# A two-layer diffusion trunk on one core: modulation weights in a ring of their own, and no pass called for at a feed-forward's turn

## The chip, the cores and the metric

One Trainium2 chip, and one core of it. The metric is the device time of one execution in microseconds, median over the runs. The engines go by the profile's names: PE is TensorE's matmuls and PEld its weight loads, DVE is VectorE, ACT ScalarE, POOL GpSimd, SP SyncE, whose queue issues the DMAs of the weights.

## What is computed

A latent stream of 256 tokens and a context of 256 tokens, 1024 channels each, go through two layers. A layer is a half-step feed-forward, four token mixers that are merged by gates, and another half-step feed-forward. Cut to what matters here:

```python
mod_x = (silu(c) @ w_ada[l] + b_ada[l]).reshape(c.shape[0], 1, 3, 3, D_MODEL)
mod_c = (silu(c_ctx) @ w_ada[l] + b_ada[l]).reshape(3, 3, D_MODEL)

def swiglu_ffn(h, w_in, w_out):
    a = h @ w_in
    return (silu(a[..., :D_FF]) * a[..., D_FF:]) @ w_out

def gated_merge(branches, pg, w_branch, w_out):
    ys = stack(branches, axis=2)
    proj = einsum('bnim,imd->bnid', ys, w_branch)
    gate = sigmoid(pg.reshape(B, N, N_BRANCH, D_MODEL))
    return sum(gate * proj, axis=2) @ w_out

x = residual(x, swiglu_ffn(modulate(x, mod_x, 0), ffn_w_in[l, 0], ffn_w_out[l, 0]), mod_x, 0, ...)
```

The modulation (`mod_x`, `mod_c`) is a product of two vectors with a matrix of 1024 x 9216 for each layer: shift, scale and gate of the three sub-layers. The sub-layers are called (l, s) below, with s = 0 for the first feed-forward, 1 for the mixers, 2 for the second feed-forward; feed-forwards are called (l, w).

## The kernel before

**Layout.** Channels lie on the partitions: eight tiles of 128 channels with 512 columns, 256 of the context and 256 of the latent stream. In layer 1 the second feed-forward and most of the mixers work on the latent columns alone.

**Matrix products in three terms.** Every operand is split into a high and a low part, and `mm3` (L149 and on) issues three matmuls: high times high, high times the low part of the activations, low part of the weights times high. `wload` loads a weight block of 128 x 1024 (`raw`), ACT makes `hi` from it (`split`, L125) and DVE makes `lo` (L113). Rings: four buffers for `raw`, six each for `hi` and `lo`. Products go into five banks of PSUM (`mm`) and three more (`ax`).

**Feed-forward** (`ffn`, from L524). The 22 blocks of the hidden layer are worked in three parts, `PARTS = ((0, 6), (6, 14), (14, 22))`. In each part the input tiles come first: two weight blocks per tile, 48 matmuls; then ACT makes silu (`sg`), DVE multiplies it by the other half (the product, `sg<-sg,mm`), ACT makes the high part (`gh<-sg`) and DVE the low part (`gh<-sg,gh`). This is called a gate below. Then come the eight output tiles over all gates of the part (`out_tiles`), each added to the residual stream by DVE (`ah<-mm,gate,ah`). The step from the last gate of a part to its first output tile is called a turn: turn 1 to 3. Output tile 0 needs the last gate last: PE works through the older gates of the part first.

**Mixer** (`mixer`, ends at L1165). In its last phase `merge` makes eight gated products for each of the four branches; for each of these 32, called a merge below, DVE multiplies (`th<-th,mm`) and adds (`mg<-mg,th`). Then the eight sums are split (`mh`, high part on ACT, low part on DVE), and the output projection (`o2`) follows.

**Modulation passes.** The modulation isn't done on PE but on DVE, beside the rest. `mods(l, s)` (from L206) is a generator: for each 128 rows of the modulation matrix it loads a block of 128 x 1024 (`ada`, L214) and makes two passes over it, one for each vector (`junk<-ada,cbc`, L216), a product with a running sum:

```python
w = wp.tile([128, D], F32, tag="raw", name=nm("ada"), bufs=4)
nc.sync.dma_start(w, I["wada"][l, s * 24 + t])
for v in range(2):
    V.tensor_tensor_reduce(out=cur["junk"], in0=w, in1=cur["c"][:, v], ...)
    yield
```

`pump(n)` takes n passes from the generators that are queued. `ffn` calls `pump(np_)` after each gate (L551) and `pump(nm_)` after each output tile (L561), with `PUMPS = ((3, 3), (3, 0), (3, 1))` for the feed-forwards (0,0), (0,1) and (1,0). Layer 0 has 112 passes, which go with feed-forward (0,0); layer 1 has 144, queued ahead of feed-forward (0,1); (1,1) has none. `ada` blocks share the ring of four with all weight blocks.

**What sets the order.** The code issues instructions in program order, but a scheduler of the framework then orders each engine's rows anew: a row may move ahead of others where nothing that it needs holds it (its buffer, its data). The queue of SP issues DMAs in its order, and a DMA waits there for its buffer to be free.

Of the kernel before, what the change touches and what calls it, by code (L numbers as in the profile page):

```python
# [10 lines left out]
F32 = mybir.dt.float32  # L11
# [5 lines left out]
D = 1024  # L17
# [43 lines left out]
def trunk_kernel(ctx: ExitStack, tc: tile.TileContext, I: dict, out: bass.AP):  # L61
# [71 lines left out]
            stt(out=lo, in0=src, scalar=scale, in1=hi.bitcast(F32), op0=ALU.mult, op1=ALU.subtract)  # L133

    def wload(ap, n=1024):
        raw = wp.tile([128, 1024], F32, tag="raw", name=nm("raw"), bufs=4)
        nc.sync.dma_start(raw[:, :n], ap)
        hi = wp.tile([128, 1024], F32R, tag="hi", name=nm("hi"), bufs=6)
        lo = wp.tile([128, 1024], F32R, tag="lo", name=nm("lo"), bufs=6)
        split(hi[:, :n], lo[:, :n], raw[:, :n])  # L140
        return hi, lo
# [65 lines left out]
    def mods(l, s):  # L207
        m = const.tile([128, 2, 24], F32, name=f"mod{l}{s}")
        mod[l, s] = m
        first = (l, s) == (0, 0)  # L210
        order = ([] if first else [c * 8 + k for k in range(8) for c in (1, 0)]) + [16 + k for k in range(8)]
        for n, t in enumerate(order):
            w = wp.tile([128, D], F32, tag="raw", name=nm("ada"), bufs=4)
            nc.sync.dma_start(w, I["wada"][l, s * 24 + t])  # L214
            for v in range(2):
                V.tensor_tensor_reduce(out=cur["junk"], in0=w, in1=cur["c"][:, v], scale=1.0, scalar=0.0,  # L216
                                       op0=ALU.mult, op1=ALU.add, accum_out=m[:, v, t:t + 1])
                yield
            if n == 15 and not first:
                g = const.tile([128, 2, 8], F32, name=f"gp{l}{s}")  # L220
                b = const.tile([128, 2, 8], F32, name=f"bp{l}{s}")
                pl, pk = (l, s - 1) if s else (l - 1, 2)
                for v in range(2):
                    sc, sh = m[:, v, 8:16], m[:, v, 0:8]
                    tt(out=sh, in0=sh, in1=col(l, "b_ada", s * 24, 8), op=ALU.add)
                    tt(out=sc, in0=sc, in1=col(l, "b_ada", s * 24 + 8, 8), op=ALU.add)
                    stt(out=g[:, v], in0=sc, scalar=1.0, in1=col(pl, "ln_g", pk * 8, 8), op0=ALU.add, op1=ALU.mult)
                    stt(out=b[:, v], in0=sc, scalar=1.0, in1=col(pl, "ln_b", pk * 8, 8), op0=ALU.add, op1=ALU.mult)
                    tt(out=b[:, v], in0=b[:, v], in1=sh, op=ALU.add)
                gp[l, s], bpc[l, s] = g, b  # L230
        gt = const.tile([128, 2, 8], F32, name=f"gate{l}{s}")
        for v in range(2):
            tt(out=gt[:, v], in0=m[:, v, 16:24], in1=col(l, "b_ada", s * 24 + 16, 8), op=ALU.add)
        if s != 1:
            ts(out=gt, in0=gt, scalar1=0.5, scalar2=None, op0=ALU.mult)
        gate[l, s] = gt
# [91 lines left out]
    def start(mid):  # L328


        xh, xl = xtiles()
        g = const.tile([128, 2, 8], F32, name="gp00")
        b = const.tile([128, 8, 2], F32, name="bp00")
        m = const.tile([128, 2, 8], F32, name="sc00")
        p = aux("shift")
        tiles, rows = [], None
        ws = {}

        def load(u):
            ws[u] = [blk("shw") for _ in range(4)]  # L340
            for i in range(4):
                nc.sync.dma_start(ws[u][i], I["wshift"][u, i])

        load(0)
        nc.sync.dma_start(cols[0], I["cols"][0])
        nc.sync.dma_start(pos, I["pos"])
        for u in range(4):
            wa = []
            for k in (2 * u, 2 * u + 1):
                wa.append(wp.tile([128, D], F32, tag="raw", name=nm("ada"), bufs=4))  # L350
                nc.sync.dma_start(wa[-1], I["wada"][0, 8 + k])
            for k in (2 * u, 2 * u + 1):
                nc.sync.dma_start(ah[k], I["xc"][k])
            if u < 3:
                load(u + 1)
            if u % 2 == 0:
                rows = aux("row")
            r = rows[0:2, (u % 2) * 256:(u % 2) * 256 + 256]
            for i in range(8):
                mm(r, ccol[:, i], ws[u][i // 2][:, (i % 2) * 256:(i % 2) * 256 + 256], start=i == 0, stop=i == 7)  # L360
            rs = blk("row")[0:2, 0:256]
            act(rs, r, AF.Copy)
            for k in (2 * u, 2 * u + 1):
                w = wa[k % 2]
                for v in range(2):
                    V.tensor_tensor_reduce(out=cur["junk"], in0=w, in1=cur["c"][:, v], scale=1.0, scalar=0.0,  # L366
                                           op0=ALU.mult, op1=ALU.add, accum_out=m[:, v, k:k + 1])
                ts(out=g[:, :, k], in0=m[:, :, k], scalar1=col(0, "b_ada", 8 + k), scalar2=1.0, op0=ALU.add, op1=ALU.add)
                mm(p[:, 2 * k:2 * k + 2], rs[:, (k % 2) * 128:(k % 2) * 128 + 128], ident[0:2, 0:2],
                                 start=True, stop=True)  # L370
                act(b[:, k], p[:, 2 * k:2 * k + 2], AF.Identity, bias=col(0, "b_ada", k))
                x3 = ah[k][:, T:].rearrange("p (r c) -> p r c", c=64)
                pk = (pos[:, 4 * k:4 * k + 4].rearrange("p (r c) -> p r c", c=1) if k < 4 else
                      pos[:, 16 + (k - 4) * 64:80 + (k - 4) * 64].rearrange("p (r c) -> p r c", r=1))
                G_.tensor_tensor(out=x3, in0=x3, in1=pk.to_broadcast([128, 4, 64]), op=ALU.add)
                xf = blk("xf")
                for v in range(2):
                    act(xf[:, vcols(v)], ah[k][:, vcols(v)], AF.Identity, scale=g[:, v, k:k + 1], bias=b[:, k, v:v + 1])
                split(xh[k], xl[k], xf)
            if u in MID:  # L380
                tiles += mid(MID.index(u))
        nc.sync.dma_start(masks, I["masks"].rearrange("d p t -> p d t"))
        nc.sync.dma_start(cols[1], I["cols"][1])
        for k in range(8):
            act(ah[k], ah[k], AF.Copy, scale=ALPHA)
        for l in range(DEPTH):
            for s in range(3):
                a = const.tile([128, 2, 8], F32, name=f"alg{l}{s}")
                ts(out=a[:, 0], in0=col(l, "ln_g", s * 8, 8), scalar1=ALPHA, scalar2=None, op0=ALU.mult)
                ts(out=a[:, 1], in0=col(l, "ln_b", s * 8, 8), scalar1=ALPHA, scalar2=None, op0=ALU.mult)  # L390
                alg[l, s] = a
        return xh, xl, tiles
# [118 lines left out]
    def first_tiles(n):  # L511
        if n < 2:
            return ffn_tiles(0, 0, (n,))
        tiles = []
        for h in range(2):
            raw = wp.tile([128, D], F32, tag="raw", name=nm("raw"), bufs=4)
            nc.sync.dma_start(raw, I["ffn_in"][0, 0, n, h])
            hi, lo = [blk("wh", F32R) for _ in range(2)], [blk("wl", F32R) for _ in range(2)]
            for i in range(2):
                split(hi[i], lo[i], raw[:, i * 512:i * 512 + 512])  # L520
            tiles.append((aux() if h else mmb(), hi, lo))
        return tiles

    def ffn(l, w, bd, first, cs, order, np_, nm_=1):  # L524
# [5 lines left out]
        for pi, (j0, j1) in enumerate(PARTS):  # L530
            gh, gl = [], []
            j = j0
            while j < j1:
# [9 lines left out]
                for i, jj in enumerate(js):  # L543
                    sg = blk("sg")
                    act(sg[:, cs], tiles[2 * i][0][:, cs], AF.Silu)
                    tt(out=sg[:, cs], in0=sg[:, cs], in1=tiles[2 * i + 1][0][:, cs], op=ALU.mult)
                    a, b = blk2("gh", cs, F32R)
                    split(a[:, cs], b[:, cs], sg[:, cs])
                    gh.append(a)
                    gl.append(b)  # L550
                    pump(np_)  # L551
                j += len(js)
            if pi == 0:
                finish_gate(l, s)
# [2 lines left out]
            def evac(m, p, c, vs):  # L557
                resid(m, p, l, s, vs)
                if fin:
                    nrm.arrive(m, c)  # L560
                pump(nm_)  # L561

            rest = out_tiles(lambda m: wload(I["ffn_out"][l, w, m, :, j0 * 128:j1 * 128], (j1 - j0) * 128),
                             gh, gl, cs, order, evac, LAG if fin and len(order) > 1 else 0)
# [9 lines left out]
    def mixer(l, bd, cs, sets, order):  # L574
# [44 lines left out]
        ready = {}  # L619

        def chunk(key):
            n = plan.index(key)
            for x in plan[n:n + 1 + AHEAD]:
                if x not in ready:
                    w = I["w_" + x[0]][l]
                    w = w[x[1] // 4, x[1] % 4] if x[0] == "br" else w[x[1]]
                    if plain(x):
                        ready[x] = wp.tile([128, 1024], F32, tag="raw", name=nm("raw"), bufs=4)
                        nc.sync.dma_start(ready[x], w)
                    else:  # L630
                        ready[x] = wload(w)
# [252 lines left out]

        def gates_v_in():

            raw = wp.tile([128, 1024], F32, tag="raw", name=nm("raw"), bufs=4)
            nc.sync.dma_start(raw[:, :128], I["w_gt"][l])
            hi = wp.tile([128, 1024], F32R, tag="hi", name=nm("hi"), bufs=6)
            lo = wp.tile([128, 1024], F32R, tag="lo", name=nm("lo"), bufs=6)  # L890
# [431 lines left out]
```

## Time and profile before

| | |
|---|---|
| runs, median (lowest to highest) | 2267.71 us (2266.44 to 2270.55) |
| profiled execution, its own time | 2267.27 us |
| its span | 2265.5 us |
| mean granted clock of TensorE | 0.991 |
| busy: PE, DVE, ACT | 98%, 72%, 42% of the span |
| DMA | 142 GB/s on the mean |

A busy time is the sum of an engine's instructions in a stretch. A wait stands at the instruction that waited, with the one that released it. The clock is the share of full speed that the chip granted to TensorE. One feed-forward with 512 columns takes some 370 us, and turn 2 of feed-forward (0,0) lies at 222 us in this execution.

### The profile page before, as it was taken

Reading aid. Unit: us, or ns where it says so; the run is one execution under the profiler, and the core shown is the slowest. Engines: PE = TensorE matmul, PEld = TensorE weight load, DVE = VectorE, ACT = ScalarE, POOL = GpSimd, SP = SyncE. Lnnn points to the kernel's source line nnn. Section 1 sums busy time; section 2 is a strip of 40 time slices with the busy share of each in tenths; the row PEclk is TensorE's granted clock in tenths of the full one; section 3 lists DMA queues with packets and bytes.
Section 4 is the critical chain, followed back from the end, with each engine's and each line's share of the span. In section 5 each row is a group of like instructions: output and inputs, shape, how many; then the busy total and the mean of one; then the engine's idle time right before and its main releaser. Section 6 shows DMA issues by size and latency. Waiting matters only on the chain.

```text
span 2265.5 us, 31565 instructions
## 1 busy us (share of the span) xinstructions
PE 2221.0 (98%) x12216; PEld 1908.4 (84%) x12216; DVE 1630.0 (72%) x2881; ACT 947.0 (42%) x1477; POOL 19.9 (1%) x82
## 2 busy tenths in 40 slices
PE   7999999999999999999999999999999999998997
PEld 4888788988888888898888888888889998998997
DVE  6998855768995754795746498766558988776656
ACT  5323123742345753362222254222226645755443
POOL 2000000000000000000000000000000000000000
PEclk9999999999999999999999999999999999999999
DMA  8676643223232132244545425554434543354652
GB/s 308 220 229 221 192 152 94 98 84 113 94 99 88 57 103 93 96 135 150 170 129 158 130 84 186 179 180 152 140 102 142 192 139 103 122 174 136 203 180 83
DMA packets 94454, 323.23 MB, mean 143 GB/s; under 512 B 10592, under 2 KB 12640, under 8 KB 94304
## 3 DMA queue, kind: packets, MB, share of 16 engines
q1 hardware_dynamic: 94304, 321.22, 43.9%
q8 instruction: 96, 1.57, 0.3%
q14 instruction: 54, 0.44, 0.1%
HBM read 320.12 MB, written 1.05 MB: 142 GB/s over the span
## 4 chain that ended last, share of the span: by engine, by line
PE 87%; DVE 7%; DMA 3%; issue 2%; ACT 2%; SPq 0%; DVEq 0%; ACTq 0%
PE mm L122 82%; DVE junk L216 2%; DMA ada<-in_wada 1%; DVE lo L113 1%; PE num L122 1%; DMA raw<-in_ffn_in 1%; DVE junk L366 1%; ACT hi L125 1%; DVE ah L113 0%; PE gt L122 0%; PE ax L122 0%; PE qk L122 0%; PE bcm L122 0%; PE bcr L122 0%; PE st L122 0%
## 5 line engine op out<-in xcount | busy, mean ns | idle before, releaser
L125 ACT ACTIVATE hi<-raw 128x1024 fp32r<-128x1024 f32 (+1 forms) x462 | 474.5, 1031 | 1040.0 <-PE mm L122 659.1
L122 PE MATMUL mm<-xh,hi 128*128 128x512 f32 (+1 forms) x2448 | 847.8, 349 | 5.0 <-ACT hi L125 3.0
L122 PE MATMUL mm<-xl,hi 128*128 128x512 f32 (+1 forms) x2448 | 850.0, 348 | 0.0
L122 PE MATMUL mm<-xh,lo 128*128 128x512 f32 (+1 forms) x2448 | 850.0, 348 | 0.0
L113 DVE TENSOR_TENSOR lo<-raw,hi 128x1024 fp32r<-128x1024 f32 (+1 forms) x462 | 546.2, 1185 | 264.6 <-ACT hi L125 262.4
L122 PEld LDWEIGHTS mm<-xh,hi 128*128 128x128 f32 x2448 | 462.4, 190 | 65.0 <-ACT hi L125 4.4
L122 PEld LDWEIGHTS mm<-xh,lo 128*128 128x128 f32 x2448 | 464.8, 190 | 58.8 <-DVE lo L113 0.4
L122 PEld LDWEIGHTS mm<-xl,hi 128*128 128x128 f32 x2448 | 465.2, 190 | 57.9 <-issue 0.7
L122 PE MATMUL mm<-gh,hi 128*128 128x512 f32 (+1 forms) x1600 | 405.8, 344 | 5.6 <-ACT gh L125 4.7
L216 DVE CUSTOM_DVE_ANT_0 junk<-ada,cbc 128x1024 bf16<-128x1024 f32 x256 | 312.9, 1222 | 107.1 <-DMA ada<-in_wada 104.0
L122 PEld LDWEIGHTS mm<-gh,hi 128*128 128x128 f32 x1600 | 276.6, 189 | 48.0 <-ACT gh L125 5.1
L122 PE MATMUL mm<-gh,lo 128*128 128x512 f32 (+1 forms) x800 | 275.5, 345 | 0.0
L122 PEld LDWEIGHTS mm<-gh,lo 128*128 128x128 f32 x800 | 150.8, 189 | 20.2 <-issue 0.7
L113 DVE SCALAR_TENSOR_TENSOR ah<-mm,gate,ah 128x256 f32<-128x256 f32 x192 | 86.4, 479 | 81.4 <-PE mm L122 81.2
L113 DVE SCALAR_TENSOR_TENSOR cacc<-pd,cw,cacc 128x512 f32<-128x512 f32 (+1 forms) x240 | 133.1, 613 | 0.2
L122 PE MATMUL mm<-yh,hi 128*128 128x512 f32 (+1 forms) x512 | 129.3, 339 | 0.1
L113 DVE TENSOR_TENSOR sg<-sg,mm 128x512 f32<-128x512 f32 (+1 forms) x87 | 53.7, 618 | 82.4 <-PE mm L122 81.7
L122 PEld LDWEIGHTS mm<-yh,hi 128*128 128x128 f32 x512 | 88.0, 189 | 11.6 <-ACT yh L125 0.3
L122 PE MATMUL mm<-yh,lo 128*128 128x512 f32 (+1 forms) x256 | 86.5, 338 | 0.0
L125 ACT ACTIVATE gh<-sg 128x512 fp32r<-128x512 f32 (+1 forms) x88 | 50.5, 574 | 76.0 <-DVE sg L113 75.5
L122 PE MATMUL mm<-mh,hi 128*128 128x256 f32 (+1 forms) x320 | 67.0, 306 | 0.5 <-ACT mh L125 0.3
L125 ACT ACTIVATE xf<-ah,bp,gp 128x256 f32<-128x256 f32 x88 | 48.8, 592 | 21.6 <-DVE ah L113 16.5
(241 smaller groups left out, 1759.6 us busy)
## 6 DMA issues: line engine op xcount, KB each, us to landing
raw<-in_ffn_in SPq DMA_DIRECT2D x176, 512.0 KB, 3.4
ada<-in_wada SPq DMA_DIRECT2D x136, 512.0 KB, 4.2
raw<-in_ffn_out SPq DMA_DIRECT2D x64, 512.0 KB, 3.7
raw<-in_w_G SPq DMA_DIRECT2D x64, 512.0 KB, 3.3
raw<-in_w_br SPq DMA_DIRECT2D x32, 512.0 KB, 3.3
raw<-in_ffn_out SPq DMA_DIRECT2D x32, 384.0 KB, 3.4
raw<-in_w_o SPq DMA_DIRECT2D x24, 512.0 KB, 3.4
shw<-in_wshift SPq DMA_DIRECT2D x16, 256.0 KB, 5.8
```

The lines of the kernel that those rows point to most:

```text
L113: return f(*a, **k)
L122: nc.tensor.matmul(o, w, x, **kw)
L125: S.activation(o, i, f, **kw)
L216: V.tensor_tensor_reduce(out=cur["junk"], in0=w, in1=cur["c"][:, v], scale=1.0, scalar=0.0, op0=ALU.mult, op1=ALU.add, accum_out=m[:, v, t ...
L366: V.tensor_tensor_reduce(out=cur["junk"], in0=w, in1=cur["c"][:, v], scale=1.0, scalar=0.0, op0=ALU.mult, op1=ALU.add, accum_out=m[:, v, k ...
```

## The change

`ada` blocks get a ring of their own with two buffers, and the ring of the weight blocks goes from four to three. In the start of the kernel, where eight modulation blocks are loaded too, the even ones use the new ring and the odd ones that of the weights. In `ffn` the passes called for after the last gate of a part and after output tile 0 are called for elsewhere: twice as many after the first gate of the part and after output tile 1. The number of passes is the same.

```diff
@@ -133,7 +133,7 @@
             stt(out=lo, in0=src, scalar=scale, in1=hi.bitcast(F32), op0=ALU.mult, op1=ALU.subtract)
 
     def wload(ap, n=1024):
-        raw = wp.tile([128, 1024], F32, tag="raw", name=nm("raw"), bufs=4)
+        raw = wp.tile([128, 1024], F32, tag="raw", name=nm("raw"), bufs=3)
         nc.sync.dma_start(raw[:, :n], ap)
         hi = wp.tile([128, 1024], F32R, tag="hi", name=nm("hi"), bufs=6)
         lo = wp.tile([128, 1024], F32R, tag="lo", name=nm("lo"), bufs=6)
@@ -210,7 +210,7 @@
         first = (l, s) == (0, 0)
         order = ([] if first else [c * 8 + k for k in range(8) for c in (1, 0)]) + [16 + k for k in range(8)]
         for n, t in enumerate(order):
-            w = wp.tile([128, D], F32, tag="raw", name=nm("ada"), bufs=4)
+            w = wp.tile([128, D], F32, tag="ada", name=nm("ada"), bufs=2)
             nc.sync.dma_start(w, I["wada"][l, s * 24 + t])
             for v in range(2):
                 V.tensor_tensor_reduce(out=cur["junk"], in0=w, in1=cur["c"][:, v], scale=1.0, scalar=0.0,
@@ -347,7 +347,7 @@
         for u in range(4):
             wa = []
             for k in (2 * u, 2 * u + 1):
-                wa.append(wp.tile([128, D], F32, tag="raw", name=nm("ada"), bufs=4))
+                wa.append(wp.tile([128, D], F32, tag=("ada", "raw")[k % 2], name=nm("ada"), bufs=2 + k % 2))
                 nc.sync.dma_start(wa[-1], I["wada"][0, 8 + k])
             for k in (2 * u, 2 * u + 1):
                 nc.sync.dma_start(ah[k], I["xc"][k])
@@ -548,7 +548,8 @@
                     split(a[:, cs], b[:, cs], sg[:, cs])
                     gh.append(a)
                     gl.append(b)
-                    pump(np_)
+
+                    pump(0 if jj == j1 - 1 else np_ * 2 if jj == j0 else np_)
                 j += len(js)
             if pi == 0:
                 finish_gate(l, s)
@@ -558,7 +559,7 @@
                 resid(m, p, l, s, vs)
                 if fin:
                     nrm.arrive(m, c)
-                pump(nm_)
+                pump(0 if m == 0 else nm_ * 2 if m == 1 else nm_)
 
             rest = out_tiles(lambda m: wload(I["ffn_out"][l, w, m, :, j0 * 128:j1 * 128], (j1 - j0) * 128),
                              gh, gl, cs, order, evac, LAG if fin and len(order) > 1 else 0)
...
```

What is left out are three more places where `bufs=4` becomes `bufs=3` for a `raw` tile.

The order of DVE, at three places. Names: `junk` with `ada` is a pass (its second row, `mod`, reads the sum), `lo<-raw,hi` a weight split, `sg` a product, `gh` a low part.

First, turn 2 of feed-forward (0,0), before: from the last pair of passes ahead of the product of gate 13 to the first output tile.

```order
L216 ISA junk_98,mod_1685<-ada_1920,cbc_93 128x1024
L216 ISA mod_1685 128x1
L113 TENSOR_TENSOR sg_1674<-sg_1674,mm_1625 128x512
L113 TENSOR_TENSOR lo_1889<-raw_1886,hi_1888 128x1024
L113 TENSOR_TENSOR gh_1678<-sg_1674,gh_1677 128x512
L216 ISA junk_98,mod_1685<-ada_1957,cbc_93 128x1024
L216 ISA mod_1685 128x1
L216 ISA junk_98,mod_1685<-ada_1957,cbc_93 128x1024
L216 ISA mod_1685 128x1
L216 ISA junk_98,mod_1685<-ada_1961,cbc_93 128x1024
L216 ISA mod_1685 128x1
L113 SCALAR_TENSOR_TENSOR ah_102<-mm_1696,gate_801,ah_102 128x256 x2
```

The same stretch with the change:

```order
L216 ISA junk_98,mod_1616<-ada_1961,cbc_93 128x1024
L216 ISA mod_1616 128x1
L113 TENSOR_TENSOR sg_1683<-sg_1683,mm_1634 128x512
L216 ISA junk_98,mod_1616<-ada_1961,cbc_93 128x1024
L216 ISA mod_1616 128x1
L113 TENSOR_TENSOR gh_1687<-sg_1683,gh_1686 128x512
L113 TENSOR_TENSOR lo_1889<-raw_1886,hi_1888 128x1024
L216 ISA junk_98,mod_1616<-ada_1998,cbc_93 128x1024
L216 ISA mod_1616 128x1
L216 ISA junk_98,mod_1616<-ada_1998,cbc_93 128x1024
L216 ISA mod_1616 128x1
L113 SCALAR_TENSOR_TENSOR ah_102<-mm_1696,gate_732,ah_102 128x256 x2
```

Six passes stand between the products of gates 12 and 13 in both. Behind the last product came a weight split and then the low part; now a pass comes, then the low part, then the split. Behind the low part stand two passes in place of three.

Second, where mixer 0 turns from its merges to its output projection, before: from the product of the last merge but one.

```order
L113 SCALAR_TENSOR_TENSOR th_7300<-th_7300,mm_7287 128x512
L113 TENSOR_TENSOR mg_4226<-mg_4226,th_7300 128x512
L113 TENSOR_TENSOR lo_7472<-raw_7469,hi_7471 128x1024
L113 SCALAR_TENSOR_TENSOR mh_7353<-mg_3889,mh_7352 128x512
L113 TENSOR_SCALAR hbg_13399<-cols_100 128x32
L113 SCALAR_TENSOR_TENSOR mh_7357<-mg_3890,mh_7356 128x512
L113 SCALAR_TENSOR_TENSOR th_7348<-th_7348,mm_7335 128x512
L113 TENSOR_TENSOR lo_7509<-raw_7506,hi_7508 128x1024
L113 TENSOR_TENSOR mg_4227<-mg_4227,th_7348 128x512
L113 SCALAR_TENSOR_TENSOR mh_7361<-mg_3995,mh_7360 128x512
L113 SCALAR_TENSOR_TENSOR mh_7365<-mg_3996,mh_7364 128x512
L113 SCALAR_TENSOR_TENSOR mh_7369<-mg_4110,mh_7368 128x512
```

With the change, from the sum of the last merge but one:

```order
L113 TENSOR_TENSOR mg_4226<-mg_4226,th_7300 128x512
L216 ISA junk_7682,mod_9758<-ada_9909,cbc_7677 128x1024
L216 ISA mod_9758 128x1
L216 ISA junk_7682,mod_9758<-ada_9909,cbc_7677 128x1024
L216 ISA mod_9758 128x1
L216 ISA junk_7682,mod_9758<-ada_9913,cbc_7677 128x1024
L216 ISA mod_9758 128x1
L113 TENSOR_TENSOR lo_7472<-raw_7469,hi_7471 128x1024
L113 SCALAR_TENSOR_TENSOR mh_7353<-mg_3889,mh_7352 128x512
L113 SCALAR_TENSOR_TENSOR th_7348<-th_7348,mm_7335 128x512
L113 SCALAR_TENSOR_TENSOR mh_7357<-mg_3890,mh_7356 128x512
L113 TENSOR_TENSOR mg_4227<-mg_4227,th_7348 128x512
```

Three passes of layer 1 now stand between this sum and the first of the low parts `mh`, and one in front of each of the last four. Up to the product before, there are 57 passes inside the last 16 merges, where there were none.

Third, turn 1 of feed-forward (0,1), before: from the product of gate 4 to the low part of gate 5.

```order
L113 TENSOR_TENSOR sg_8424<-sg_8424,mm_8375 128x512
L113 TENSOR_TENSOR lo_8596<-raw_8593,hi_8595 128x768
L113 TENSOR_TENSOR gh_8428<-sg_8424,gh_8427 128x512
L113 TENSOR_TENSOR lo_8623<-raw_8620,hi_8622 128x768
L113 TENSOR_TENSOR sg_8500<-sg_8500,mm_8451 128x512
L113 TENSOR_TENSOR lo_8650<-raw_8647,hi_8649 128x768
L113 TENSOR_TENSOR gh_8504<-sg_8500,gh_8503 128x512
```

With the change, the same place from the second of these splits on; three of the seven passes between the two products stand ahead of it:

```order
L113 TENSOR_TENSOR lo_8623<-raw_8620,hi_8622 128x768
L216 ISA junk_7682,mod_9758<-ada_11497,cbc_7677 128x1024
L216 ISA mod_9758 128x1
L216 ISA junk_7682,mod_9758<-ada_11497,cbc_7677 128x1024
L216 ISA mod_9758 128x1
L216 ISA junk_7682,mod_9758<-ada_11555,cbc_7677 128x1024
L216 ISA mod_9758 128x1
L216 ISA junk_7682,mod_9758<-ada_11555,cbc_7677 128x1024
L216 ISA mod_9758 128x1
L113 TENSOR_TENSOR sg_8505<-sg_8505,mm_8456 128x512
L113 TENSOR_TENSOR lo_8650<-raw_8647,hi_8649 128x768
L113 TENSOR_TENSOR gh_8509<-sg_8505,gh_8508 128x512
```

No pass stood between the last products of the part; now six, six and seven stand before gates 3, 4 and 5 of the part. All passes of layer 1 are over by gate 12 of this feed-forward; before, 78 of them came in feed-forward (1,0).

## Rows read from the trace of the kernel before

**Rows 1.** The page: PE's busy time (share of the span) xinstructions; the chain that ended last.
```profile
PE 2221.0 (98%) x12216; PEld 1908.4 (84%) x12216; DVE 1630.0 (72%) x2881; ACT 947.0 (42%) x1477; POOL 19.9 (1%) x82
...
PE 87%; DVE 7%; DMA 3%; issue 2%; ACT 2%; SPq 0%; DVEq 0%; ACTq 0%
```

**Rows 2.** Waits of PE in 54 to 240 us: total us, times, longest us.
```profile
PE mm L122 <- ACT gh L125: 4.7, 1, 4.7
```

**Rows 3.** Busy us (instructions) by stretch: PE, PEld, DVE, ACT, POOL, clock, DMA.
```profile
54.00:225.00 171.00, 170.54 (x748) 140.02 (x747) 157.98 (x261) 52.08 (x66) 0.00 (x0) 1.00 0.69 223
870.00:940.00 70.00, 70.00 (x302) 56.18 (x301) 32.19 (x42) 22.15 (x29) 0.00 (x0) 1.00 0.29 96
1360.00:1680.00 320.00, 320.00 (x1445) 264.30 (x1444) 209.21 (x326) 97.97 (x128) 0.13 (x1) 1.00 0.50 160
```

**Rows 4.** Timeline of PE at the second turn: start us, length us, [wait <- releaser].
```profile
222.22 0.63 PE L122 MATMUL mm<-gh,hi 128*128 128x512 f32 x2
226.87 0.40 PE L122 MATMUL mm<-gh,lo 128*128 128x512 f32 x1
231.93 0.80 PE L122 MATMUL mm<-gh,hi 128*128 128x512 f32 x1 [4.65 <-ACT gh L125]
233.00 0.79 PE L122 MATMUL mm<-gh,hi 128*128 128x512 f32 x1 [0.28 <-DVE gh L113]
239.02 0.63 PE L122 MATMUL mm<-gh,hi 128*128 128x512 f32 x2
```

**Rows 5.** Busy times and granted clock behind and beside two idle times of PE.
```profile
232.00:234.00 2.00, 1.72 (x3) 1.04 (x4) 2.00 (x3) 0.12 (x1) 0.00 (x0) 0.50 0.86 240
...
20.00:22.00 2.00, 0.00 (x0) 0.00 (x0) 1.07 (x2) 2.00 (x4) 0.00 (x0) 1.00 1.07 398
22.00:24.00 2.00, 1.58 (x4) 1.05 (x5) 1.83 (x3) 2.00 (x4) 0.36 (x1) 0.57 0.97 352
```

**Rows 6.** Timeline of DVE in part 2 of the first feed-forward.
```profile
147.74 0.68 DVE L113 TENSOR_TENSOR sg<-sg,mm 128x512 f32<-128x512 f32 x1
...
228.11 1.23 DVE L216 CUSTOM_DVE_ANT_0 junk<-ada,cbc 128x1024 bf16<-128x1024 f32 x1 [0.83 <-DMA ada<-in_wada]
229.38 1.22 DVE L216 CUSTOM_DVE_ANT_0 junk<-ada,cbc 128x1024 bf16<-128x1024 f32 x1
230.53 0.68 DVE L113 TENSOR_TENSOR sg<-sg,mm 128x512 f32<-128x512 f32 x1
231.13 1.22 DVE L113 TENSOR_TENSOR lo<-raw,hi 128x1024 fp32r<-128x1024 f32 x1
232.26 0.68 DVE L113 TENSOR_TENSOR gh<-sg,gh 128x512 fp32r<-128x512 f32 x1
```

**Rows 7.** Instructions of DVE by form, 54 to 240 us: busy us, mean ns.
```profile
L113 DVE TENSOR_TENSOR lo<-raw,hi 128x768 fp32r<-128x768 f32 x8 | 7.6, 954 | 0.5 <-ACT hi L125 0.5
```

**Rows 8.** DMA issues in 54:240, then in 870:940: count, KB, median us to landing.
```profile
ada<-in_wada SPq DMA_DIRECT2D x42, 512.0 KB, 4.2
raw<-in_ffn_in SPq DMA_DIRECT2D x24, 512.0 KB, 4.3
...
raw<-in_w_o SPq DMA_DIRECT2D x8, 512.0 KB, 3.3
```

**Rows 9.** Timeline of DVE: gates at the first turn of feed-forward (0,1).
```profile
1034.36 0.69 DVE L113 TENSOR_TENSOR sg<-sg,mm 128x512 f32<-128x512 f32 x1 [3.85 <-PE mm L122]
1045.24 0.69 DVE L113 TENSOR_TENSOR sg<-sg,mm 128x512 f32<-128x512 f32 x1 [3.85 <-PE mm L122]
```

**Rows 10.** Timelines at the end of mixer 0: DVE's products, PE's first output matmul.
```profile
902.52 0.69 DVE L113 SCALAR_TENSOR_TENSOR th<-th,mm 128x512 f32<-128x512 f32 x1 [0.80 <-PE mm L122]
919.13 0.69 DVE L113 SCALAR_TENSOR_TENSOR th<-th,mm 128x512 f32<-128x512 f32 x1 [0.80 <-PE mm L122]
...
927.17 0.63 PE L122 MATMUL mm<-mh,hi 128*128 128x512 f32 x2
```

**Rows 11.** The page's costliest groups: the high parts of the weights on ACT.
```profile
L125 ACT ACTIVATE hi<-raw 128x1024 fp32r<-128x1024 f32 (+1 forms) x462 | 474.5, 1031 | 1040.0 <-PE mm L122 659.1
```

More of the change, by code (lines that the diff above doesn't have):

```diff
@@ L515, in first_tiles @@
         for h in range(2):
-            raw = wp.tile([128, D], F32, tag="raw", name=nm("raw"), bufs=4)
+            raw = wp.tile([128, D], F32, tag="raw", name=nm("raw"), bufs=3)
             nc.sync.dma_start(raw, I["ffn_in"][0, 0, n, h])
@@ L627, in chunk @@
                     if plain(x):
-                        ready[x] = wp.tile([128, 1024], F32, tag="raw", name=nm("raw"), bufs=4)
+                        ready[x] = wp.tile([128, 1024], F32, tag="raw", name=nm("raw"), bufs=3)
                         nc.sync.dma_start(ready[x], w)
@@ L885, in gates_v_in @@
         def gates_v_in():
-            raw = wp.tile([128, 1024], F32, tag="raw", name=nm("raw"), bufs=4)
+            raw = wp.tile([128, 1024], F32, tag="raw", name=nm("raw"), bufs=3)
             nc.sync.dma_start(raw[:, :128], I["w_gt"][l])
```

## The prediction

> **What bounds the kernel now.** I read the page's busy times and its chain first. TensorE works 2221.0 us of the span, and the chain that ended last is PE for 87% [rows 1]; a microsecond counts only where TensorE stops. Next come TensorE's waits in the first feed-forward: one wait of 4.7 us for the activation that makes a gate's high part [rows 2]. The busy times by stage then say where VectorE is short of time: it works 157.98 of 171 us there, but 32.19 of 70 in the merges of mixer 0 and 209.21 of 320 in feed-forward (1,0), and in these two TensorE is busy all the time [rows 3]. So one place can give something back, the turn at 222 us, and several can lose.
>
> What that turn costs: its input tiles end at 222.2, and 20 matmuls on seven older gates run to 226.87, 0.2325 us each. The last gate's high part should go in at 227.1 and its low part at 227.33; they go in at 231.93 and 233.00. The matmul that starts at 239.02 is the 19th after 226.87 and would have started at 226.87 + 19 x 0.2325 = 231.3 [rows 4]. The loss is 7.7 us: 5.3 of waiting (233.00 less 227.33, and less what the one matmul between was slowed) and 2.4 because the granted clock stood at 0.50 for some microseconds behind the wait, the lower of its two levels [rows 5]. The cause stands on VectorE: the last gate's product starts at 230.53, 8.3 us after its tile was done, and a pass before it had waited 0.83 us for its weights [rows 6].
>
> **What the change does at the turns.** The order of VectorE's rows, not the source, decides. In the first feed-forward six passes still stand between the last two gates of part 2, as before; the moved calls put one pass between the last product and its low part, in place of a weight split. The lever is the ring. A pass's weights now wait for the pass before last to end, no longer for weight splits, and the passes of layer 1 run ahead: 57 of them fall into the last 16 merges of mixer 0, and all are done in the second part of feed-forward (0,1), so that (1,0) has none.
>
> Prices, start to start [rows 6]: a pass 1.27 us before another pass, 1.15 before anything else; a weight split 1.13; a product or a gate's low part 0.60. A split of 768 columns is 0.87 (its 0.95 busy less the 0.08 by which neighbours overlap) [rows 7].
>
> The unknown is the time from freed buffer to landed weights, since two buffers leave about two passes for it. Nearest rows: 4.2 us for these loads and 4.3 for the others in the first feed-forward, 3.3 for weights that load alone [rows 8]. I take 4.3, because each load still has others 1 to 3 us around it, and keep 3.5 and 4.6 as ends.
>
> *Turn 2 of the first feed-forward.* Per tile: six passes 3 x 1.27 + 3 x 1.15 = 7.26, two splits 2.26, product and low part 1.20: 10.72 against TensorE's 10.88 [rows 9]. One load per tile has only two passes and a split to land in, 1.27 + 1.15 + 1.13 = 3.55, so VectorE waits 0.75 and falls behind by 0.59 per tile. The second gate of the part was 1.7 late before (147.74 against 222.2 - 7 x 10.88 = 146.0) [rows 6]; I take 1.3 now, and seven tiles later 5.4. The last product starts at 227.6, the high part follows at +1.40 as before, at 229.0, 1.9 late; the low part at +2.5, at 230.1, 0.9 later still. Loss 2.8 with the clock kept, against 7.7: **-4.9**. At a landing of 3.5 nothing is left (-7.7), at 4.6 the wait is 4.9 and the clock falls: -0.4.
>
> *Where mixer 0 turns from its merges to its output projection.* Before, VectorE was half idle here; the order now shows eight passes per pair of merges. A pair takes 16.6 us (902.52 to 919.13) [rows 10]: passes 9.7, three splits 3.4, four products 2.4, together 15.5; but loads that have a product and two passes to land in (0.6 + 2.5 = 3.1) wait 1.2 each, two per pair at times. That is up to 1.3 late per pair, about 3 at the last merge but one, whose product was at 919.13 [rows 10]. From 922.1: product 0.6, pass 1.15, sum 0.6, three passes 3.7, a wait of 1.2, a split 1.13 and the first low part 0.6 give 931.1. TensorE begins the projection at 927.17 [rows 10] and wants that low part at its fourth matmul, 927.9: a wait of 3.2 us. TensorE did nothing in 20 to 22 us, and then the clock was at 0.57 [rows 5]; I charge 1.7, between the 0.9 that those two microseconds lost and the 2.4 of turn 2. **+4.9** (ends 0 and +7.2). Passes between the later low parts keep pace with TensorE, one each 1.75 us.
>
> *First turn of feed-forward (0,1).* The last three gates of part 1 had no pass before them, and VectorE waited for TensorE (3.85 us at two of them [rows 9]). Now six, six and seven passes stand there. Twice +0.6 as above; the last tile is seven passes 8.6, two short splits 1.7, 1.2, and a wait of 1.0 (3.3 to land in), 12.6 in all: +1.7. From 0.6 the last product comes 3.5 late, at 1048.6, and the low part at +2.07, at 1050.7, where 15 matmuls and one more cover until 1048.9: **+1.8**, clock kept (ends 0 and +4.4).
>
> *At nothing.* Turn 1 of the first feed-forward: 24 passes in place of 25 before the gate, 0.6 us at most either way. Feed-forward (1,0) loses 78 passes, 97 us of VectorE, but TensorE was busy 320.00 of 320 us there [rows 3]. Three buffers for weights: a buffer's round is 4.3 to land, 1.03 for the high part [rows 11] and 1.2 for the low, 6.5 over three, 2.2 us per tile against 5.4 of TensorE. SyncE's queue: each load stands in it in the order in which VectorE frees the buffers, so none holds back the next by its place.
>
> Sum: -4.9 + 4.9 + 1.8 = +1.8 on the profiled execution's 2267.27 (the median of the runs is 2267.71): **2269.2 us**, which is no change that a measurement of this kernel can tell, about 0.2% or 4.5 us.
>
> **Rivals.**
> *Faster: the loads land in time.* At 3.5 to 3.9 us from release to landing the ring of two suffices: turn 2 closes (-7.7), the merges cost 0 to 1.2, turn (0,1) 0 to 0.7. 2259.6 to 2261.5, and 2261 is the value. For it: weights that load alone take 3.3 [rows 8], and one ring frees its buffers evenly. Against it: the stretches in question had 4.2. The Trainium skill ("DMA: Bandwidth & Descriptors", Anatomy of one DMA) gives 2.0 us fixed plus bytes over 436 GB/s, 3.2 us for 512 KB, which is a fit for another issuing path. By that figure this rival would come true; the trace agrees with it for a load by itself and not for loads beside others.
>
> *Slower: VectorE is the bound at three turns.* From 4.5 us on, turn 2 keeps its wait and its slow clock (-0.4 at 4.6), the projection of mixer 0 waits 5.5 and loses 1.7 of clock (+7.2), turn (0,1) 2.7 and 1.7 (+4.4): +11, 2278.5. For it: 38 of 70 us were free on VectorE in the merges before [rows 3], and now next to none are. Against it: the passes could wait less where no load stands right ahead.
>
> *The change does not do what it says.* Six passes stay between the last two gates of the turn that counts. If the lag comes from them and the ring changes nothing, turn 2 costs its 7.7 again and the passes run in idle time elsewhere: 2267.3. Against it: the waits for the pass weights (0.83 at the turn alone [rows 6]) come from the shared ring.
>
> **How the numbers follow.** The forecast covers landings of 4.0 to 4.4, -3.5 to +6 us: 0.49, of which 0.37 lies within 0.2%, 0.03 faster and 0.09 slower. Loads in time: 0.23, of which 0.22 faster. Bound by VectorE: 0.18, all slower. Nothing changes: 0.10, all the same. Faster 0.25, the same 0.48, slower 0.27. The range takes in most of both outer cases: 2260 to 2278.
>
> **What would show it.** Right: at turn 2 the last product some 5 us behind its tile and a wait for the high part of 1 to 3 us with the clock at 1.00; a new wait of TensorE for a low part of the merged product, about 3 us, where mixer 0 begins its output projection; one of about 2 us at the first turn of (0,1); waits of VectorE for pass weights of 0.5 to 1.2 us each in the merges. Wrong: no wait at either new place while VectorE's passes there wait less than 0.3 us (the loads are in time), or the old 4.7 us still at turn 2. A wait that I did not name, at a place where passes were hoisted to, would make the sum wrong in its kind.

## The result, and the profile after

The change made the kernel slower: 2287.57 us, median of 4 runs (2286.01 to 2288.82), against 2267.25 (2266.44 to 2270.55). The ratio is 1.0093, with a 95% interval from 1.0079 to 1.0107. That is 20 us more where 2 were forecast, and 9.6 us above the upper end of the range.

The first lines of the page after:

```profile
span 2284.0 us, 31582 instructions
...
PE 2227.6 (98%) x12216; PEld 1911.2 (84%) x12216; DVE 1628.2 (71%) x2881; ACT 946.6 (41%) x1477; POOL 19.0 (1%) x82
...
PE 82%; DVE 9%; DMA 4%; issue 2%; ACT 2%; DVEq 0%; SPq 0%; ACTq 0%
```

TensorE has the same 12216 matmuls. Its share of the chain fell from 87% to 82% of the span, while VectorE's rose from 7% to 9% and the DMAs' from 3% to 4% [rows 1]. Where that lies is read best from the starts of the same ACT instruction in both traces (silu of a gate, tanh of a merge; the first feed-forward's end is PE's statistic):

| place | before | after | later by |
|---|---|---|---|
| feed-forward (0,0), gate 13 (last before turn 2) | 221.11 | 221.24 | 0.1 |
| its end | 398.13 | 399.17 | 1.0 |
| mixer 0, merge 16 | 804.92 | 805.96 | 1.0 |
| mixer 0, merge 31 (the last) | 925.28 | 928.23 | 2.9 |
| feed-forward (0,1), gate 5 (last before turn 1) | 1040.30 | 1046.09 | 5.8 |
| gate 6 (first behind turn 1) | 1084.59 | 1096.32 | 11.7 |
| feed-forward (1,0), its last gate | 1662.53 | 1673.80 | 11.3 |
| mixer 1, merge 0 | 1758.33 | 1773.33 | 15.0 |
| feed-forward (1,1), gate 0 | 2073.53 | 2092.11 | 18.6 |

So there are four results: turn 2 gave nothing back (+1.0 over the first feed-forward), 4.8 us went from merge 16 to gate 5 of (0,1), 5.9 at the turn behind it, and 7.3 in mixer 1, where the prediction put the cost at nothing.

**Turn 2.** VectorE's timeline after, in part 2 of the first feed-forward, from its first product to its last:

```profile
147.43 0.68 DVE L113 TENSOR_TENSOR sg<-sg,mm 128x512 f32<-128x512 f32 x1
...
170.36 1.23 DVE L216 CUSTOM_DVE_ANT_0 junk<-ada,cbc 128x1024 bf16<-128x1024 f32 x1 [1.76 <-DMA ada<-in_wada]
...
215.06 1.23 DVE L216 CUSTOM_DVE_ANT_0 junk<-ada,cbc 128x1024 bf16<-128x1024 f32 x1 [0.85 <-DMA ada<-in_wada]
...
217.88 1.23 DVE L216 CUSTOM_DVE_ANT_0 junk<-ada,cbc 128x1024 bf16<-128x1024 f32 x1 [0.32 <-DMA ada<-in_wada]
219.03 0.68 DVE L113 TENSOR_TENSOR sg<-sg,mm 128x512 f32<-128x512 f32 x1
...
227.07 1.22 DVE L216 CUSTOM_DVE_ANT_0 junk<-ada,cbc 128x1024 bf16<-128x1024 f32 x1 [0.81 <-DMA ada<-in_wada]
...
230.80 0.68 DVE L113 TENSOR_TENSOR sg<-sg,mm 128x512 f32<-128x512 f32 x1
```

and TensorE's from the end of its input tiles, with the waits:

```profile
223.00 0.63 PE L122 MATMUL mm<-gh,hi 128*128 128x512 f32 x2
...
232.20 0.58 PE L122 MATMUL mm<-gh,hi 128*128 128x512 f32 x1 [4.15 <-ACT gh L125]
233.28 0.80 PE L122 MATMUL mm<-gh,hi 128*128 128x512 f32 x1 [0.50 <-DVE gh L113]
```

and the clock behind them:

```profile
234.00:236.00 2.00, 2.00 (x6) 1.53 (x5) 1.97 (x4) 1.06 (x1) 0.00 (x0) 0.50 0.71 250
```

A tile takes VectorE 11.9 us, the mean of the seven from 147.43 to 230.80, against TensorE's 10.88. Each of them has waits for the passes' weights, 0.5 to 1.8 us per tile and 7.3 us in all; in three tiles there are two such waits. The input tiles end at 223.00, 0.8 us later than before, so 0.8 of the +1.0 was lost ahead of the turn. The last product starts at 230.80, 7.8 us behind its tile where it was 8.3 before [rows 4, rows 6]. The wait is 4.15 where it was 4.65 [rows 4], and the clock behind it is at 0.50 as before. The passes' blocks land in 4.3 us (median of the 45 issued from 54 to 240 us).

**End of mixer 0.** TensorE's two waits, in the merges and at the first matmuls of the output projection:

```profile
869.61 0.50 PE L122 MATMUL mm<-yh,hi 128*128 128x512 f32 x1 [0.80 <-DVE yh L113]
...
932.88 0.50 PE L122 MATMUL mm<-mh,hi 128*128 128x512 f32 x1 [1.90 <-DVE mh L113]
```

VectorE's busy time in the stretch that had 32.19 of 70 us before [rows 3], and the clock behind the second wait:

```profile
870.00:940.00 70.00, 68.00 (x294) 54.61 (x293) 66.16 (x114) 19.98 (x26) 0.00 (x0) 1.00 0.63 205
...
932.00:934.00 2.00, 1.12 (x5) 0.86 (x5) 2.00 (x5) 1.74 (x4) 0.00 (x0) 1.00 0.36 92
```

It is now nearly full, with 66.16. The clock stayed at 1.00 behind a wait of 1.90.

**First turn of (0,1).** VectorE's last tile, then TensorE, then the clock:

```profile
1043.66 0.68 DVE L113 TENSOR_TENSOR sg<-sg,mm 128x512 f32<-128x512 f32 x1
...
1051.32 1.23 DVE L216 CUSTOM_DVE_ANT_0 junk<-ada,cbc 128x1024 bf16<-128x1024 f32 x1 [0.95 <-DMA ada<-in_wada]
...
1056.44 0.68 DVE L113 TENSOR_TENSOR sg<-sg,mm 128x512 f32<-128x512 f32 x1
```

```profile
1050.75 0.63 PE L122 MATMUL mm<-gh,hi 128*128 128x512 f32 x2
...
1057.84 0.50 PE L122 MATMUL mm<-gh,hi 128*128 128x512 f32 x1 [3.46 <-ACT gh L125]
1058.65 0.79 PE L122 MATMUL mm<-gh,hi 128*128 128x512 f32 x1 [0.31 <-DVE gh L113]
```

```profile
1056.00:1058.00 2.00, 0.16 (x1) 0.16 (x1) 2.00 (x5) 0.63 (x1) 0.00 (x0) 1.00 0.50 143
1058.00:1060.00 2.00, 1.69 (x4) 1.18 (x5) 1.83 (x4) 0.47 (x1) 0.00 (x0) 0.63 0.83 279
1060.00:1062.00 2.00, 2.00 (x6) 1.52 (x6) 2.00 (x4) 0.37 (x1) 0.00 (x0) 0.52 0.58 203
```

The input tiles end at 1050.75 and the last product starts at 1056.44, 5.7 us later. Before, VectorE waited 3.85 us for TensorE at this gate [rows 9]. TensorE waits 3.46, and in the four microseconds from 1058 on the clock is lower (0.63, then 0.52).

**Mixer 1.** It has no passes in either kernel. ACT's waits for weight blocks from the last gate of (1,0) to merge 16 of mixer 1, before:

```profile
ACT hi L125 <- DMA raw<-in_w_G: 1.5, 2, 0.8
ACT hi L125 <- DMA raw<-in_w_Ba: 0.3, 1, 0.3
```

and after:

```profile
ACT hi L125 <- DMA raw<-in_w_G: 3.1, 3, 1.5
ACT hi L125 <- DMA raw<-in_w_br: 2.3, 3, 1.0
ACT hi L125 <- DMA raw<-in_w_Au: 1.9, 1, 1.9
ACT hi L125 <- DMA raw<-in_w_Bg: 1.2, 1, 1.2
ACT hi L125 <- DMA raw<-in_w_k: 0.3, 1, 0.3
ACT hi L125 <- DMA raw<-in_w_v: 0.2, 1, 0.2
```

1.8 us became 9.0. The issues in SyncE's queue show where it begins. The first pair of gate weights, before:

```profile
1737.47 1.84 SPq L137 DMA_DIRECT2D raw<-in_w_G  x2
```

and after:

```profile
1752.86 1.80 SPq L137 DMA_DIRECT2D raw<-in_w_G  x2
```

TensorE's work of that time comes 11.3 us later in the trace after, so this pair should go out at 1748.8; it goes out 4.1 us behind that. With three buffers the queue is one block shorter throughout. In the wide feed-forward tiles that hides in TensorE's 5.4 us per block; in mixer 1, with 256 columns, blocks are taken two and three in a row. One wait of TensorE there, before:

```profile
1949.29 0.49 PE L122 MATMUL C<-vaug,kw 128*128 128x129 f32 x2 [0.34 <-ACT kw L125]
```

and its two longest new ones, after:

```profile
1772.11 0.38 PE L122 MATMUL mm<-yh,hi 128*128 128x256 f32 x1 [1.97 <-ACT yh L125]
...
1967.84 1.26 PE L122 MATMUL C<-vaug,kw 128*128 128x129 f32 x8 [3.20 <-ACT kw L125]
```

The first of the two stands behind the late blocks: by merge 0, 3.7 of the 7.3 us are lost. How the second comes about is not shown. ACT waits for no weight block between 1883 us and it, yet TensorE's lateness grows from 15.1 us at 1895 to 18.6 there.

### The profile page after: what moved, and what is told of

Its sections match the earlier page's. It is cut to its first block, busy times and chain, and to the rows that moved or that the text cites. A ratio compares the mean times of both kernels' runs of the same rounds, so it can differ in the third digit from the quotient of the medians.

```text
span 2284.0 us, 31582 instructions
## 1 busy us (share of the span) xinstructions
PE 2227.6 (98%) x12216; PEld 1911.2 (84%) x12216; DVE 1628.2 (71%) x2881; ACT 946.6 (41%) x1477; POOL 19.0 (1%) x82
## 3 DMA queue, kind: packets, MB, share of 16 engines
HBM read 320.12 MB, written 1.05 MB: 141 GB/s over the span
## 4 chain that ended last, share of the span: by engine, by line
PE 82%; DVE 9%; DMA 4%; issue 2%; ACT 2%; DVEq 0%; SPq 0%; ACTq 0%
PE mm L122 77%; DMA ada<-in_wada 4%; DVE junk L216 3%; DVE lo L113 2%; PE num L122 1%; DVE junk L366 1%; ACT hi L125 1%; PE gt L122 0%; PE ax L122 0%; DVE gh L113 0%; DVE sg L113 0%; PE qk L122 0%; DMA raw<-in_w_br 0%; PE bcm L122 0%; PE bcr L122 0%
## 5 line engine op out<-in xcount | busy, mean ns | idle before, releaser
L122 PEld LDWEIGHTS mm<-mh,hi 128*128 128x128 f32 x320 | 51.4, 188 | 7.0 <-DVE mh L113 2.8
```

What stands on the lines that cost most here:

```text
L122: nc.tensor.matmul(o, w, x, **kw)
```

## The experiments

Each of the ten is timed beside the kernel before on the same chip. The table gives, for each run's profiled execution, how much later or earlier than before it is over four stretches (same instructions as above; in us): feed-forward (0,0); from there to gate 6 of (0,1); from there to the last gate of (1,0); mixer 1. Two runs whose order is nearly the same, the change and the rings alone, differ by 2 to 4 us in a stretch, so smaller numbers than that are not read.

| kernel | (0,0) | to gate 6 of (0,1) | to end of (1,0) | mixer 1 | median | ratio to before, 95% |
|---|---|---|---|---|---|---|
| the change | +1.0 | +10.7 | -0.5 | +7.3 | 2287.57 | 1.0079 to 1.0107 |
| rings alone | -1.2 | +15.0 | -0.5 | +5.8 | 2289.13 | 1.0084 to 1.0116 |
| calls alone | +0.8 | +1.0 | +0.6 | -0.7 | 2270.08 | 1.0005 to 1.0024 |
| layer 1 shared | +1.6 | -0.9 | +0.4 | +8.0 | 2276.07 | 1.0025 to 1.0055 |
| one ring of three | +3.8 | -0.3 | +1.2 | +8.8 | 2282.61 | 1.0052 to 1.0090 |
| weights four | -0.4 | +9.1 | -1.0 | -3.3 | 2274.41 | 1.0021 to 1.0045 |
| own ring of three | -7.8 | +2.3 | -0.9 | +6.7 | 2268.80 | 1.0001 to 1.0020 |
| own three, weights four | -8.1 | +3.0 | -0.5 | -2.9 | 2259.07 | 0.9943 to 0.9978 |
| two passes per gate | -6.1 | -0.1 | 0.0 | -0.5 | 2259.76 | 0.9959 to 0.9981 |
| the same, 32 blocks | -5.0 | +0.6 | +0.7 | -1.8 | 2261.68 | 0.9975 to 0.9994 |
| the same, ring of five | -6.4 | +1.9 | -0.5 | -2.6 | 2262.69 | 0.9969 to 0.9989 |

**Rings alone: which half of the change acts?**

```diff
-                    pump(0 if jj == j1 - 1 else np_ * 2 if jj == j0 else np_)
+                    pump(np_)
...
-                pump(0 if m == 0 else nm_ * 2 if m == 1 else nm_)
+                pump(nm_)
```

> The two rings without the moved calls. The order of the rows is that of the change but for four rows on VectorE. Theory: the moved calls do nothing beside the rings, 2287.5 us as the change. Rival: the few rows that the calls move at turns are worth some us: outside 2285 to 2290.

2289.13 us: the rings are the change, and beside them the moved calls are worth nothing that shows. Here too 55 passes fall into the last 16 merges of mixer 0: with a ring of their own, the scheduler takes passes early, wherever the code calls for them.

**Calls alone.** The kernel before, with the two changed lines of `ffn` and its ring of four.

> The moved calls without the rings (one shared ring of four). The order still has six passes between the last two products before turn 2, and one pass more before the last product at turn 1. Theory: the wait at turn 2 stays, since the lag comes from the passes before it, and the time is 2267, at most 2 us off. Rival: the passes that the calls keep from the turn shorten it by more than 4 us: 2263 or less.

2270.08 us, 4.2 above the kernel before beside it (2265.9). Expected were 2267 us, at most 2 off, with the wait at turn 2 still there; both were missed. The doubled calls behind the first gate of part 1 delay a weight split there:

```profile
75.42 0.79 PE L122 MATMUL mm<-xh,lo 128*128 128x512 f32 x1 [4.39 <-DVE lo L113]
```

TensorE falls back by that wait (7.7 us at gate 5), VectorE is then no longer behind it, and the wait at turn 2 is gone (gate 13 is 5.2 later than before, gate 14 only 0.8). A wait was moved from one place to another.

**Layer 1 in the weights' ring.**

```diff
-            w = wp.tile([128, D], F32, tag="ada", name=nm("ada"), bufs=2)
+            w = wp.tile([128, D], F32, tag=("ada", "raw")[l], name=nm("ada"), bufs=2 + l)
```

> The change, but only layer 0's modulation blocks have the own ring of two; those of layer 1 share the ring of three with the weights, so their passes cannot run ahead into mixer 0. Theory: the 10.7 us at the end of mixer 0 and at the first turn of feed-forward (0,1) go, mixer 1 keeps its 7.1: 2277 us. Rival: those waits come from loads being slower with two rings and not from passes that run ahead: 2287 us.

2276.07 us. No pass falls into the last 16 merges, and the second stretch is at -0.9: the 10.7 us come with the passes that run ahead. Mixer 1 keeps its loss, with the same two waits of TensorE (1.97 and 3.20).

**One ring of three.** The kernel before with `bufs=3` for `raw` and `ada`.

> The kernel before with one thing changed: the shared ring has three buffers in place of four. Theory: mixer 1, which has no passes, loses its 7.1 us here too, and the stretch from mixer 0 to feed-forward (0,1) loses nothing, since the passes of layer 1 cannot run ahead: 2274 us, more if the first feed-forward waits longer for its passes. Rival: mixer 1 is as before, 2267 us.

Mixer 1 loses 8.8 us with no second ring in the kernel: it is the depth of the weights' ring. The median is 8.6 us above what was expected, of which the profile shows 3.8 in the first feed-forward (the shared ring is shorter for passes too); its own execution was the second fastest of four.

**Weights four, own ring of two.**

```diff
-        raw = wp.tile([128, 1024], F32, tag="raw", name=nm("raw"), bufs=3)
+        raw = wp.tile([128, 1024], F32, tag="raw", name=nm("raw"), bufs=4)
...
-    bp = ctx.enter_context(tc.tile_pool(name="bp", bufs=33))
+    bp = ctx.enter_context(tc.tile_pool(name="bp", bufs=32))
```

> The change with four buffers for the weights again, beside the own ring of two (paid for by one of the 33 general blocks). Theory: the 7.1 us that mixer 1 lost come from the weights' ring of three, whose loads start 4 to 5 us later there; they go, the 10.7 at the end of mixer 0 and at the first turn of feed-forward (0,1) stay: about 2280 us, with mixer 1 as long as before. Rival: mixer 1 lost them to the order in which the rows reached it, not to the ring: 2287 us. A third: the missing general block costs by itself, 2287 or more.

2274.41 us, 5.6 less than expected: mixer 1's loss is gone, and 3.3 us more than that, which was not expected; the second stretch keeps 9.1. Over all kernels of the table, mixer 1 loses 5.8 to 8.8 us with three buffers for weights, with the same two waits of TensorE in each trace (1.97 or 1.98, and 3.20), and nothing with four or five.

**Own ring of three, weights three.** The change with `bufs=3` for `ada`, and 32 general blocks.

> The change with three buffers in the ring of the modulation blocks in place of two (the weights keep three; 32 general blocks in place of 33). Theory: with two buffers a load has only about two passes to land in, and it takes longer; with three it has over 6 us, so VectorE's waits for pass weights go (they were 0.3 to 0.85 us, two per tile), the lag at turn 2 and the wait there go (-7.7 us), and of the 10.7 us at the end of mixer 0 and the first turn of (0,1) more than half goes; mixer 1 keeps its 7 us: about 2272 us. Rival: six passes per gate are too many for VectorE whatever the ring, and the time stays at 2285 or more.

2268.80 us, 3 less than expected. In the first feed-forward neither TensorE nor VectorE waits for a pass any more; all of VectorE's waits from 54 to 240 us are

```profile
DVE ah L113 <- PE mm L122: 0.9, 1, 0.9
DVE sg L113 <- PE mm L122: 0.5, 1, 0.5
```

It has six passes per gate as the change has, and now waits for TensorE. So the two buffers kept turn 2 open, where six passes per gate alone don't; the missing general block is not the reason, since the run before has 32 too and stays at -0.4. The second stretch falls from 10.7 to 2.3, though 58 passes still fall into the last 16 merges: running ahead was costly with two buffers, and nearly free with three.

**Both rings larger.** The change with `bufs=3` for `ada`, `bufs=4` for `raw`, 31 general blocks and five padded ones in place of six.

> Both rings larger than in the change: three buffers for the modulation blocks and four for the weights (paid for by two of the 33 general blocks and one of six padded ones). Theory: all three causes are then gone but for what the passes that run ahead cost by their number: turn 2 gives back 7.8, the end of mixer 0 and the first turn of (0,1) cost 1.4 together, mixer 1 is as long as before: 2261 us. Rival: mixer 1 keeps a loss of 6 to 7 us with four buffers too, since it comes from the rings being apart: 2268.

2259.07 us, faster than before by 0.22 to 0.57%. ACT's waits for weights in the stretch in mixer 1 that had 1.8 us before and 9.0 with the change:

```profile
ACT hi L125 <- DMA raw<-in_w_Ba: 0.2, 1, 0.2
```

**Two passes per gate.**

```diff
-PUMPS = ((3, 3), (3, 0), (3, 1))
+PUMPS = ((2, 3), (3, 0), (3, 1))
```

> The kernel before with its shared ring of four, and two passes called for after each gate of the first feed-forward in place of three; the order has 28 passes between the second and the ninth gate of its second and third part, where there were 36. Theory: VectorE keeps up with TensorE there, the wait of 4.7 us at turn 2 and the slow clock behind it go, and the passes find room later: 7.7 us less, 2259.6. Rival: the lag comes back at the third turn or where the mixer begins, and the time stays at 2267.

2259.76 us. TensorE's waits from 54 to 240 us:

```profile
PE mm L122 <- DVE gh L113: 1.0, 2, 0.6
PE mm L122 <- ACT gh L125: 0.7, 1, 0.7
```

The wait of 4.7 us [rows 2] is 0.7. One number in the kernel before is worth what both larger rings are, without their memory.

**Two controls.** Two passes per gate with 32 general blocks in place of 33:

> Two passes per gate in the first feed-forward as in the run before (2259.8 us), and 32 general blocks in place of 33, with nothing else changed. This is the control for the two runs that pay for a buffer with such a block; in the first of them mixer 1 was 3.3 us shorter than before. Theory: the block is the reason: 2256.5 us, with mixer 1 shorter by 3. Rival: the block does nothing and mixer 1 varies by that from run to run: 2260 us.

2261.68 us: the expected 2256.5 did not come. Mixer 1 is shorter by 1.8, and in all four runs with fewer blocks and four or five buffers for weights it is shorter than in the two with 33 blocks and four (-0.5 and -0.7). But these differences are of the size that is not read here, and the whole is no faster, so what the block does stays open. And a ring of five, with 31 blocks:

> Two passes per gate and a shared ring of five in place of four (31 general blocks). It asks whether four buffers for weights still bind where three cost 7 us. Theory: with four the narrow tiles of mixer 1 still wait now and then for a weight block (0.3 to 0.7 us at the high parts), so five give 1 to 3 us there: 2257 to 2259. Rival: four are enough and mixer 1 is as long as with four, 2260.

2262.69 us: no gain, four buffers are enough.

## Why the prediction was wrong

**What bounds the kernel** was read rightly: the one place with something to give was turn 2, and its 7.7 us can be had (-7.8 with the own ring of three, -6.1 with two passes per gate).

**Turn 2 (-4.9): mis-sized, +1.0 by the end of the feed-forward.** The step that failed is "One load per tile has only two passes and a split to land in", with a wait of 0.75 per tile. The trace shows 1.05 us of waits per tile (7.3 over seven), three times with a second one of 0.3 to 0.5 at a load that was taken for covered; and the rest of a tile takes 10.86, where 10.72 had been added up. VectorE starts the part 0.6 late, not 1.3, but falls behind by 1.03 us per tile, not by 0.59, and is 7.8 late at the turn, not 5.4. The wait then was 4.15, and the clock, forecast as kept, fell. The mechanism was right, and the run with three buffers shows it: about the same passes, no wait. My end of the range, a landing of 4.6, gave -0.4. (147.74 is the product of the part's first gate and not of its second; the sum counts seven tiles from it, as it should.)

**End of mixer 0 (+4.9): +4.8, in other parts than said.** The wait for the first low part came, but was 1.90 and not 3.2, and the charge of 1.7 for the clock did not fall due. The passes between the low parts of the last branch's inputs made TensorE wait as well (0.80 at 869.61), and merge 31 was already 1.9 later than merge 16; that the prediction did not name. Nor did it name a wait of 0.83 us at 985.98 for the high part of the normalized stream (`xh`), behind the projection. That the sum came out is luck.

**First turn of (0,1) (+1.8): mis-sized, +5.9.** "From 0.6 the last product comes 3.5 late": it came 5.7 late. VectorE was behind by 2.8 us already at gate 3, where 1.2 were forecast (its product was at 1031.83, and its tile had ended two tiles ahead of 1050.75, at 1029.0), and ten small operations at the end of a generator, at 1030.6 to 1038.8, had no price (about 0.08 us each, start to start). The wait was 3.46 and the clock fell behind it, which the prediction had excluded here and charged in mixer 0.

**Three buffers for weights (put at nothing): the step that failed outright, +7.3 in mixer 1.** The prediction set a buffer's round of 6.5 us over three against the 5.4 us that TensorE takes per block of a wide tile. A mean over the feed-forward says nothing of a stage that takes several blocks at once with tiles half as wide. One ring of three alone, with all else as before, shows 8.8; four buffers take it away. No rival had it either: all three turned on the passes, and so did the range.

Sum: 1.0 + 4.8 + 5.9 + 7.3, and -0.5 from gate 6 of (0,1) to the end of (1,0), is 18.5, which is what the last gates of the two traces lie apart.

The faster rival's rule (2.0 us and bytes over 436 GB/s, the Trainium skill, "DMA: Bandwidth & Descriptors", Anatomy of one DMA, a fit for loads that GpSimd issues) gives an estimate of 3.2 us for 512 KB. Loads beside others took longer here: 4.3 us in the first feed-forward. In the merges of mixer 0 the passes' loads come near it (3.3 us, median of 16) and the weights' don't (4.4, median of 8).

## What to carry to other kernels

A ring's depth is how far ahead its loads run, so price it in the stage that takes blocks in bursts, and not by a mean round against a mean tile; three in place of four cost 7 us where the mean said nothing. A ring of its own frees background work to run ahead into any idle time that the scheduler sees, and where the code calls for it then no longer matters: follow where the rows go, and what turns lie there. What this cost hung on the ring's depth: 9 to 15 us with two buffers, 2 to 3 with three. Two buffers for work that takes 1.2 us a pass don't cover a load of 4.3; a third did. Asking for fewer passes where the engine was full gained as much.

## What was not expected of the hardware

TensorE's clock stayed at 1.00 behind a wait of 1.90 us and stood at 0.63 and 0.52 behind one of 3.46; behind the idle time at 20 to 22 us it had been 0.57 [rows 5]. A block of 512 KB took longer with another just ahead of it: the output projection's weights took 3.3 us alone in the merges before [rows 8], and 4.4 with the passes' loads beside them. Of the loads that went out from 870 to 940 us after, those issued 1.1 to 1.8 us behind another took 4.2 to 4.7 us, those 3.0 or more behind it 3.2 to 3.8.
